# Up biases of a mixture of experts: products on TensorE, or a broadcast and adds on GpSimd

## The chip, the cores and the metric

The kernel runs on one core of a Trainium2 chip. The metric is the device time of one execution in microseconds: the median of three runs.

## The reference

One layer of an encoder for 512 rows of 1024 features: layer norm, a mixer (latent attention beside a gated recurrence, one output projection), layer norm, and a mixture of 32 experts of which each row takes four. All in float32.

```python
hb = xb @ w_up[e] + b_up[e]                     # 1024 -> 2048
glu, lin = jnp.split(hb, 2, axis=-1)
glu = jnp.minimum(glu, 7.0)
lin = jnp.clip(lin, -7.0, 7.0)
act = glu * jax.nn.sigmoid(1.702 * glu) * (lin + 1.0)
y = act @ w_down[e] + b_down[e]                 # 1024 -> 1024, then times the gate, added to the row
```

The change touches how `b_up[e]` comes into `hb`, and how the rows of `w_down[e]` lie on the partitions.

## The kernel before, in words

Some 345 us go to the mixer, the second norm and the routing. The expert stage follows: for each expert one block of 128 slots, 32 for each quarter of the rows (a loop for what overflows a quarter runs as often as the counts ask for). The rows of a block are gathered from DRAM by an indirect DMA on GpSimd's queue (`fetch`, line 388), transposed by TensorE and split into a high part in fp32r and the rest (`x_T`). The weights are split in the same way: `Stream` loads chunks of 128x2048 float32 (1 MB) on SyncE's queue into raw buffers (`w_raw`; four, four and `RAW_C` of two, ten in all), ScalarE copies the high part (line 88) and VectorE subtracts it from the raw chunk (line 90, raw and high part both in SBUF), with four buffers for each part. A raw buffer that VectorE has read is loaded again at once. A product of full precision is then three products of TensorE (lines 410 to 412): high by high, high part of x by low part of w, low by high.

An expert has eight chunks of `w_up` (four sums of 128x512 in PSUM, twelve products a chunk) and four of `w_down` (two sums, twelve products a chunk; a chunk has two rows of `w_down` to a partition, p and 128 + p of its 256). The biases `b_up` of all experts lie in SBUF as three bfloat16 pieces to a row (`prepare_up`, at the end of the mixer); a product with a column of ones at the expert's three rows starts each of the four up sums (`bias_mm`, line 415).

The order of the work on every engine in the expert stage is written out by hand: `experts` runs up of expert e, then down of expert e - 1. Beside the up chunks `turn` goes forward by one step a chunk (transposes of the activations of e - 1, then of the rows of e + 1, then places and gates of the next four experts now and then); beside the down chunks `halves` does the activations of e (ScalarE reads the sums for the sigmoid and for lin + 1, VectorE reads the first again for the gate, line 439, then clamps and multiplies, lines 444 and 445). After each chunk, `ahead` splits the chunk three further on. `finish` scales the down sums on ScalarE (line 473) and adds them to a DRAM table with an indirect DMA on GpSimd (line 474). When all loads have been issued, each `ahead` also takes one step of `final_tiles`, which borrows free raw buffers, has GpSimd split `b_down` and the gates (lines 497 to 502), and has TensorE transpose the latter (line 514). An instruction waits for its operands on its engine's queue, and all behind it wait too.

Of the kernel before, what the change touches and what calls it, by code (L numbers as in the profile page):

```python
# [21 lines left out]
NE = 32  # L22
# [99 lines left out]
class Consts:  # L122
    def __init__(self, nc, pool, tmp):
        self.mhalf = pool.tile([128, 4], F32, name="mhalf")
        nc.gpsimd.memset(self.mhalf, -0.5)
        nc.scalar.copy(tmp.tile([128, 4], F32, name="act_table"), self.mhalf)
        jp = tmp.tile([128, 128], I32, name="jp")
        nc.gpsimd.iota(jp, pattern=[[1, 128]], base=0, channel_multiplier=-1)
        self.ident = pool.tile([128, 128], F32, name="ident")
        nc.vector.tensor_scalar(self.ident, jp, 0.0, None, op0=ALU.is_equal)  # L130
        self.before = pool.tile([128, 128], BF, name="before")
        nc.vector.tensor_scalar(self.before, jp, 0.0, None, op0=ALU.is_gt)
        self.ones = pool.tile([128, 128], BF, name="ones")
        nc.vector.memset(self.ones, 1.0)

        self.base = pool.tile([128, 1], F32, name="base")
        for b in range(NB):
            nc.gpsimd.memset(self.base[SLB * b:SLB * b + SLB, :], BIG + 128.0 * b)
        self.slots = pool.tile([128, 128], F32, name="slots")
        nc.gpsimd.iota(self.slots, pattern=[[1, 128]], base=-int(BIG), channel_multiplier=0,  # L140
                       allow_small_or_imprecise_dtypes=True)
        self.pcol = pool.tile([128, 1], F32, name="pcol")
        nc.gpsimd.iota(self.pcol, pattern=[[0, 1]], base=0, channel_multiplier=1,
                       allow_small_or_imprecise_dtypes=True)
        self.ecol = pool.tile([128, NE], F32, name="ecol")
        nc.gpsimd.iota(self.ecol, pattern=[[1, NE]], base=0, channel_multiplier=0,
                       allow_small_or_imprecise_dtypes=True)
        self.erow = pool.tile([128, NE], F32, name="erow")
        t = tmp.tile([128, NE], F32, name="sel_t")
        nc.vector.tensor_scalar(self.erow, jp[:, :NE], 0.0, None, op0=ALU.is_equal)  # L150
        for r in (1, 2):
            nc.vector.tensor_scalar(t, jp[:, :NE], -float(r * NE), None, op0=ALU.is_equal)
            nc.vector.tensor_add(self.erow, self.erow, t)
        self.erow_b = pool.tile([128, NE], BF, name="erow_b")
        nc.vector.tensor_copy(self.erow_b, self.erow)


class Moe:
    def __init__(self, tc, ctx, a, cst, ne=NE):
# [7 lines left out]
        self.bias = ctx.enter_context(tc.tile_pool(name="moe_bias", bufs=1)).tile([128, 2048], BF, name="bias")  # L167
# [21 lines left out]
    def load_consts(self, pool):  # L189
        nc, a = self.nc, self.a  # L190
        self.wr = pool.tile([128, 8, NE], F32, name="w_router", bufs=1)
# [22 lines left out]
    @staticmethod  # L214
    def dn_src(w, k):
        return [(lambda t: t.rearrange("p (k n) -> p k n", k=2),
                 w[256 * k:256 * (k + 1), :].rearrange("(k p) n -> p k n", p=128))]
# [104 lines left out]
    def prepare_up(self, tmp):  # L322

        nc = self.nc
        nc.gpsimd.memset(self.bias[96:128], 0.0)

        bq = tmp.tile([128, 512], F32, name="prep_b")
        for q in range(4):
            nc.scalar.dma_start(bq[32 * q:32 * q + 32], self.a["b_up"][0][:, 512 * q:512 * q + 512])
        for r in range(3):  # L330
            pt = tmp.tile([128, 512], BF, name=f"prep_p{r}")
            nc.scalar.copy(pt, bq)
            if r < 2:
                nc.vector.tensor_sub(bq, bq, pt)
            for q in range(4):
                nc.scalar.dma_start(self.bias[32 * r:32 * r + 32, 512 * q:512 * q + 512],
                                    pt[32 * q:32 * q + 32, :])

    def open(self, ctx, h1, h1_pool):
# [12 lines left out]
        self.l_bufs = [self.xp.tile([128, 512], F32, name=f"act_l{i}", bufs=1) for i in range(2)]  # L352
        self.oh = self.xp.tile([128, NB, GRP, SLB], F32, name="oh", bufs=1)
# [60 lines left out]
    def bias_mm(self, ps, sel, j):  # L414
        self.nc.tensor.matmul(ps, sel, self.bias[:, 512 * j:512 * j + 512], start=True, stop=False)

    def up_begin(self, sel):
        ps = [self.ps_up.tile([128, 512], F32, name="ps_up_t") for _ in range(4)]
        for j in range(4):
            self.bias_mm(ps[j], sel, j)  # L420
        return ps

    def up_chunk(self, ps, x, w, k):
        wh, wl = w
        xh, xl = (p[:, k, :] for p in x)
        for j in range(4):
            s = slice(512 * j, 512 * j + 512)
            self.mm3(ps[j], xh, xl, wh[:, s], wl[:, s], k == 7)

    def act0(self, ps, h):  # L430

        nc = self.nc
        nc.scalar.activation(self.u_bufs[h], ps[h], AF.Sigmoid, scale=SW_ALPHA)
        nc.scalar.activation(self.l_bufs[h], ps[2 + h], AF.Copy, bias=1.0)  # L434

    def act1(self, ps, h):

        u = self.u_bufs[h]
        self.nc.vector.scalar_tensor_tensor(u, ps[h], LIMIT, u, op0=ALU.min, op1=ALU.mult)
# [7 lines left out]
    def act_T(self, h):  # L447

        nc, ah, al = self.nc, self.ah, self.al
        p = self.ps_tr.tile([128, 4, 128], F32, name="ps_tr", tag="tr")  # L450
        for i in range(4):
            nc.tensor.transpose(p[:, i, :], self.l_bufs[h][:, 128 * i:128 * i + 128], self.c.ident)  # L452
# [122 lines left out]
    def sel_of(self, e):  # L575
        return self.c.erow_b[:, e:e + 1].to_broadcast([128, 128])

    def experts(self, out):
# [17 lines left out]
        def halves(ps):  # L596

            self.act0(ps, 0)
            self.act1(ps, 0)
            yield  # L600
            self.act0(ps, 1)
            self.act1(ps, 1)
            yield
            self.act2(0)
            yield
            self.act2(1)
            yield

        def turn():

            if e:
                t = [self.act_T(h) for h in range(2)]
                next(t[0])
# [5 lines left out]
                yield  # L619
# [14 lines left out]

        slots(0)
# [5 lines left out]
        for e in range(ne + 1):  # L641
            first = e == 0
            steps = turn()
            if e < ne:
# [3 lines left out]
                ps_up = self.up_begin(self.sel_of(e))  # L648
# [36 lines left out]
    def overflow(self, out):  # L685
# [3 lines left out]
        with tc.For_i(0, n, 1) as i:  # L689
# [26 lines left out]
            et = self.xp.tile([128, NE], F32, name="ov_et")  # L716
            nc.vector.tensor_mul(et, self.c.erow, em)
            sc = self.xp.tile([128, 1], F32, name="ov_sc")
            nc.vector.tensor_reduce(sc, et, axis=AX.X, op=ALU.add)
            sel_t = self.xp.tile([128, 1], BF, name="ov_sel")  # L720
            nc.vector.tensor_copy(sel_t, sc)
            sel = sel_t.to_broadcast([128, 128])
# [6 lines left out]
            ps = self.up_begin(sel)  # L729
            for k in range(8):  # L730
                self.up_chunk(ps, self.x[0], chunk(self.up_src(wu, k)), k)
            for h in range(2):
                self.act0(ps, h)
                self.act1(ps, h)
# [680 lines left out]
def run_mixer(tc, ctx, a, c, moe, st):  # L1415
# [152 lines left out]
    with ExitStack() as tst:  # L1568
        moe.prepare_up(pool(tst, "mx_btmp", side="left"))
# [55 lines left out]
RAW_C = 2  # L1625
# [10 lines left out]
def build(tc, a, out):  # L1636
    nc = tc.nc
    with ExitStack() as ctx:
# [5 lines left out]
        st.first = [st.add(*Moe.dn_src(a["w_o"][0], k)) for k in range(4)]  # L1644
# [8 lines left out]
        with ExitStack() as c2:  # L1653
# [44 lines left out]
            def keep_warm():  # L1698

                p = pj.tile([128, 512], F32, name="warm", tag="s")  # L1700
                for _ in range(B_ORDER.count("x")):
                    nc.tensor.matmul(p, c.ones, moe.bias[:, 0:512], start=True, stop=True)
# [33 lines left out]
```

## Time and profile before

| | |
|---|---|
| runs, us | 1536.73, 1534.72, 1534.84; median 1534.84 |
| profiled execution, us | 1533.35, its span 1531.5 |
| busy share of the span | TensorE 96%, VectorE 87%, ScalarE 70%, GpSimd 17% |
| packets on SyncE's queue | 86002, 425.51 MB, 74.1% of 16 engines' span |
| granted TensorE clock | 0.983 of full speed over the span |

The page gives busy time per engine over the span; a stage has to be asked for by itself. Products on TensorE overlap, so the sum of their durations is more than the time that they take, and the distance from one start to the next is what counts. The list of waits gives, for each instruction that found its engine idle, what ended the idle time.

### The profile page before, as it was taken

What the parts mean: (1) busy time and instruction counts of PE and PEld (TensorE: products, weight loads), DVE (VectorE), ACT (ScalarE), POOL (GpSimd) and SP (SyncE); (2) the same over time, 40 slices, a digit from 0 to 9 for tenths busy, and PEclk for the clock granted to TensorE, in tenths of its full rate; (3) what the DMA queues carried; (4) which work ended last, traced back from release to release, by engine and by line L of the source; (5) the groups of instructions that cost most, each with busy time, mean ns of one, the idle gap of its engine ahead of it and who ended that gap; (6) DMA issues with size and microseconds to landing.
All of it is one profiled execution on the core that took longest, in us unless ns stands there. A gap on an engine that the chain in (4) does not pass through costs nothing. (4 is left out here: it accounts for less than half of the span.)

```text
span 1531.5 us, 20026 instructions
## 1 busy us (share of the span) xinstructions
PE 1467.2 (96%) x7368; PEld 1210.5 (79%) x7401; DVE 1325.0 (87%) x1520; ACT 1072.9 (70%) x1148; POOL 259.4 (17%) x251
## 2 busy tenths in 40 slices
PE   7999999979999999999999999999999999999984
PEld 5878998857888888888888888888888888888863
DVE  8867876667999999999999989999999999998975
ACT  4778453336777777777777777777777777777762
POOL 5120413141111111111111111111101111111033
PEclk9999999999999999999999999999999999999997
DMA  5222116376999999999999999999999999999943
GB/s 200 91 76 56 29 51 256 139 262 238 337 362 366 377 364 367 371 373 366 372 374 363 363 372 364 355 383 367 379 357 371 375 367 364 378 368 359 360 150 115
DMA packets 100729, 457.15 MB, mean 298 GB/s; under 512 B 14031, under 2 KB 24696, under 8 KB 67858
## 3 DMA queue, kind: packets, MB, share of 16 engines
q1 hardware_dynamic: 86002, 425.51, 74.1%
q0 software_dynamic: 12672, 29.50, 6.6%
q8 instruction: 60, 0.98, 0.3%
q10 hardware_dynamic: 1952, 0.80, 0.2%
q14 instruction: 43, 0.35, 0.1%
HBM read 447.26 MB, written 24.64 MB: 308 GB/s over the span
## 5 line engine op out<-in xcount | busy, mean ns | idle before, releaser
L90 DVE TENSOR_TENSOR w_lo_t<-w_raw,w_hi_t 128x2048 fp32r<-128x2048 f32 (+1 forms) x392 | 880.8, 2267 | 89.9 <-ACT w_hi_t L88 89.0
L88 ACT CAST w_hi_t<-w_raw 128x2048 fp32r<-128x2048 f32 (+1 forms) x392 | 725.4, 1896 | 13.9 <-DMA w_raw<-in_w_o 12.2
L410 PE MATMUL ps_up_t<-w_hi_t,xh 128*128 128x512 f32 x1024 | 420.1, 410 | 0.0
L412 PE MATMUL ps_up_t<-w_hi_t,xl 128*128 128x512 f32 x1024 | 403.2, 394 | 0.0
L411 PE MATMUL ps_up_t<-w_lo_t,xh 128*128 128x512 f32 x1024 | 399.9, 390 | 0.0
L474 POOL DMA_INDIRECT acc_dram<-h,idx x31 | 95.5, 3081 | 956.4 <-ACT h L473 749.8
L412 PEld LDWEIGHTS ps_up_t<-w_hi_t,xl 128*128 128x128 f32 x1024 | 192.5, 188 | 43.5
L410 PEld LDWEIGHTS ps_up_t<-w_hi_t,xh 128*128 128x128 f32 x1024 | 193.1, 189 | 39.5 <-issue 0.8
L411 PEld LDWEIGHTS ps_up_t<-w_lo_t,xh 128*128 128x128 f32 x1024 | 193.5, 189 | 37.3
L412 PE MATMUL ps_dn_t<-w_hi_t,h 128*128 128x512 f32 x512 | 200.5, 392 | 1.2 <-DVE h L456 1.2
L410 PE MATMUL ps_dn_t<-w_hi_t,h 128*128 128x512 f32 x512 | 200.7, 392 | 0.2 <-ACT h L455 0.2
L411 PE MATMUL ps_dn_t<-w_lo_t,h 128*128 128x512 f32 x512 | 200.6, 392 | 0.0
L412 PEld LDWEIGHTS ps_dn_t<-w_hi_t,h 128*128 128x128 f32 x512 | 97.0, 189 | 21.8 <-DVE h L456 1.6
L410 PEld LDWEIGHTS ps_dn_t<-w_hi_t,h 128*128 128x128 f32 x512 | 96.9, 189 | 20.6 <-ACT h L455 0.4
L411 PEld LDWEIGHTS ps_dn_t<-w_lo_t,h 128*128 128x128 f32 x512 | 96.8, 189 | 20.2
L404 ACT CAST xh<-ps_tr 128x512 fp32r<-128x512 f32 x64 | 37.7, 588 | 94.9 <-PE ps_tr L401 94.7
L455 ACT CAST h<-ps_tr 128x512 fp32r<-128x512 f32 x64 | 37.5, 588 | 79.6 <-PE ps_tr L452 79.6
L473 ACT ACTIVATE h<-ps_dn_t,gate_s 128x512 f32<-128x512 f32 x62 | 42.4, 688 | 65.0 <-PE ps_dn_t L412 65.0
L940 PE MATMUL pj<-mw_hi,hT 128*128 128x256 f32 (+1 forms) x192 | 59.9, 312 | 1.9 <-ACT hT L1061 1.5
L941 PE MATMUL pj<-mw_lo,hT 128*128 128x256 f32 (+1 forms) x192 | 58.0, 303 | 1.1 <-DVE mw_lo L868 1.1
L942 PE MATMUL pj<-mw_hi,hT 128*128 128x256 f32 (+1 forms) x192 | 57.8, 301 | 0.8 <-DVE hT L1063 0.8
L434 ACT ACTIVATE act_l<-ps_up_t 128x512 f32<-128x512 f32 x64 | 38.5, 601 | 23.7 <-PE ps_up_t L412 23.7
(363 smaller groups left out, 1804.8 us busy)
## 6 DMA issues: line engine op xcount, KB each, us to landing
w_raw<-in_w_up SPq DMA_DIRECT2D x256, 1024.0 KB
w_raw<-in_w_down SPq DMA_DIRECT2D x128, 1024.0 KB
mw_raw<-in_w_in SPq DMA_DIRECT2D x16, 512.0 KB
w_raw<-in_w_o SPq DMA_DIRECT2D x4, 1024.0 KB
mw_raw<-in_w_in SPq DMA_DIRECT2D x4, 672.0 KB
h_dram<-x POOLq DMA_DIRECT2D x4, 512.0 KB, 3.5
h<-h_dram POOLq DMA_DIRECT2D x4, 512.0 KB, 10.2
rows_dram<-h POOLq DMA_DIRECT2D x4, 512.0 KB, 4.5
```

The lines of the kernel that those rows point to most:

```text
L88: self.nc.scalar.copy(h[:, s], r[:, s])
L90: self.nc.vector.tensor_sub(l[:, s], r[:, s], h[:, s].bitcast(F32))
L404: nc.scalar.copy(xh[:, s, :], p)
L410: mm(ps, xh, wh, start=start, stop=False)
L411: mm(ps, xh, wl, start=False, stop=False)
L412: mm(ps, xl, wh, start=False, stop=stop)
L434: nc.scalar.activation(self.l_bufs[h], ps[2 + h], AF.Copy, bias=1.0)
L473: nc.scalar.mul(y[:, 512 * n:512 * n + 512], ps[n], gate)
L474: nc.gpsimd.indirect_dma_start(out=self.acc[:, :], out_offset=bass.IndirectOffsetOnAxis(ap=idx[:, :1], axis=0), in_=y, in_offset=None, bou ...
L940: mm(ps, xh, wh, start=start, stop=False, skip_group_check=True)
L941: mm(ps, xh, wl, start=False, stop=False, skip_group_check=True)
L942: mm(ps, xl, wh, start=False, stop=stop, skip_group_check=True)
```

## The change

GpSimd brings in the biases. One row of `b_up` is loaded as four pieces of 512 to partitions 0, 32, 64 and 96 (`bias_row`; the first on ScalarE's queue, the others on GpSimd's, an expert ahead), and GpSimd broadcasts each to 128 partitions (`bias_rows`) behind the gather. The four bias products go, with their tables. ScalarE copies all four up sums to SBUF, GpSimd adds the biases to the copies in place, and the sigmoid and the gate read these. The clamps and products move from the down stage to the first two steps of the next `turn`. A chunk of `w_down` is loaded with rows 2p and 2p + 1 on partition p, so the transposes of the activations read every second element. `RAW_C` is one, for nine raw buffers in all. Where TensorE was kept busy with products of the bias table before the expert stage, it now multiplies ones. The overflow loop changes in the same manner.

```diff
--- before.py
+++ after.py
...
@@ class Consts: the table of expert rows goes
-        self.erow = pool.tile([128, NE], F32, name="erow")
...
-        self.erow_b = pool.tile([128, NE], BF, name="erow_b")
-        nc.vector.tensor_copy(self.erow_b, self.erow)
...
@@ class Moe
-        self.bias = ctx.enter_context(tc.tile_pool(name="moe_bias", bufs=1)).tile([128, 2048], BF, name="bias")
+        self.bias_pool = ctx.enter_context(tc.tile_pool(name="moe_bias", bufs=2))
...
     def load_consts(self, pool):
         nc, a = self.nc, self.a
+        self.brow0 = self.bias_row(a["b_up"][0, 0:1], nc.scalar)
...
     def dn_src(w, k):
+        return [(lambda t: t, w[256 * k:256 * (k + 1), :].rearrange("(p two) n -> p (two n)", two=2))]
+
+    @staticmethod
+    def out_src(w, k):
         return [(lambda t: t.rearrange("p (k n) -> p k n", k=2),
                  w[256 * k:256 * (k + 1), :].rearrange("(k p) n -> p k n", p=128))]
...
-    def prepare_up(self, tmp):
...
+    def bias_row(self, src, queue):
+
+        t = self.bias_pool.tile([128, 512], F32, name="bias_q")
         for q in range(4):
...
+            queue.dma_start(t[32 * q:32 * q + 1, :], src[:, 512 * q:512 * q + 512])
+        return t
+
+    def bias_rows(self, t):
+
+        self.bias = self.xp.tile([128, 2048], F32, name="bias", bufs=1)
+        for q in range(4):
+            self.nc.gpsimd.partition_broadcast(self.bias[:, 512 * q:512 * q + 512], t[32 * q:32 * q + 1, :])
...
+        self.s_buf = self.xp.tile([128, 512], F32, name="act_s", bufs=1)
...
-    def bias_mm(self, ps, sel, j):
-        self.nc.tensor.matmul(ps, sel, self.bias[:, 512 * j:512 * j + 512], start=True, stop=False)
-
-    def up_begin(self, sel):
-        ps = [self.ps_up.tile([128, 512], F32, name="ps_up_t") for _ in range(4)]
-        for j in range(4):
-            self.bias_mm(ps[j], sel, j)
-        return ps
+    def up_begin(self):
+        return [self.ps_up.tile([128, 512], F32, name="ps_up_t") for _ in range(4)]
...
-            self.mm3(ps[j], xh, xl, wh[:, s], wl[:, s], k == 7)
+            self.mm3(ps[j], xh, xl, wh[:, s], wl[:, s], k == 7, start=k == 0)
-
-    def act0(self, ps, h):
-
-        nc = self.nc
-        nc.scalar.activation(self.u_bufs[h], ps[h], AF.Sigmoid, scale=SW_ALPHA)
-        nc.scalar.activation(self.l_bufs[h], ps[2 + h], AF.Copy, bias=1.0)
-
-    def act1(self, ps, h):
-
-        u = self.u_bufs[h]
-        self.nc.vector.scalar_tensor_tensor(u, ps[h], LIMIT, u, op0=ALU.min, op1=ALU.mult)
+    def act0(self, ps):
+
+        nc = self.nc
+        for h in range(2):
+            for j, t in ((h, self.u_bufs[h]), (2 + h, self.l_bufs[h])):
+                if j < 2:
+                    nc.scalar.copy(t, ps[j])
+                else:
+                    nc.scalar.activation(t, ps[j], AF.Copy, bias=1.0)
+                nc.gpsimd.tensor_tensor(t, t, self.bias[:, 512 * j:512 * j + 512], op=ALU.add)
+
+    def act1(self, h):
+
+        u, s = self.u_bufs[h], self.s_buf
+        self.nc.scalar.activation(s, u, AF.Sigmoid, scale=SW_ALPHA)
+        self.nc.vector.scalar_tensor_tensor(u, u, LIMIT, s, op0=ALU.min, op1=ALU.mult)
... act_T
+        l = self.l_bufs[h].rearrange("p (k q two) -> p k two q", k=2, two=2)
         for i in range(4):
-            nc.tensor.transpose(p[:, i, :], self.l_bufs[h][:, 128 * i:128 * i + 128], self.c.ident)
+            nc.tensor.transpose(p[:, i, :], l[:, i // 2, i % 2, :], self.c.ident)
... experts: halves
-            self.act0(ps, 0)
-            self.act1(ps, 0)
-            yield
-            self.act0(ps, 1)
-            self.act1(ps, 1)
-            yield
-            self.act2(0)
-            yield
-            self.act2(1)
+            self.act0(ps)
+            yield
+            yield
+            self.act1(0)
+            yield
+            self.act1(1)
             yield
... experts: turn
                 t = [self.act_T(h) for h in range(2)]
+                self.act2(0)
+                yield
+                self.act2(1)
                 next(t[0])
                 yield
                 next(t[0])
                 next(t[1])
                 yield
                 next(t[1])
-                yield
             if e + 1 < ne:
... experts: the loop over e
+                self.bias_rows(brow)
+                if e + 1 < ne:
+                    brow = self.bias_row(self.a["b_up"][0, e + 1:e + 2], nc.gpsimd)
-                ps_up = self.up_begin(self.sel_of(e))
+                ps_up = self.up_begin()
...
-RAW_C = 2
+RAW_C = 1
```

## Rows read from the trace of the kernel before

**Rows 1.** The page: busy us of each engine (share of the span) and instructions.
```profile
PE 1467.2 (96%) x7368; PEld 1210.5 (79%) x7401; DVE 1325.0 (87%) x1520; ACT 1072.9 (70%) x1148; POOL 259.4 (17%) x251
```

**Rows 2.** Middle of the expert stage: length, busy us per engine, clock, DMA share, GB/s.
```profile
core 0: us, PE busy (x) PEld busy (x) DVE busy (x) ACT busy (x) POOL busy (x), PEclk, DMA share, GB/s
600.00:1320.00 720.00, 718.64 (x3375) 584.59 (x3394) 663.28 (x469) 555.29 (x444) 90.19 (x40) 1.00 0.99 369
```

**Rows 3.** Waits from 500 to 1400 us, longest of ScalarE, VectorE, SyncE: total, times, longest.
```profile
ACT xh L404 <- PE ps_tr L401: 64.9, 51, 1.7
...
DVE w_lo_t L90 <- ACT w_hi_t L88: 67.1, 121, 1.1
...
SPq L75 <- DVE w_lo_t L90: 628.0, 247, 3.6
```

**Rows 4.** GpSimd in order of time, two scatter-adds: start, us, engine, line [idle before].
```profile
733.70 3.00 POOL L474 DMA_INDIRECT acc_dram<-h,idx  x1 [30.24 <-ACT h L473]
...
769.26 3.01 POOL L474 DMA_INDIRECT acc_dram<-h,idx  x1 [30.79 <-ACT h L473]
```

**Rows 5.** TensorE in order of time, from one expert's down to the next one's up.
```profile
732.32 0.39 PE L412 MATMUL ps_dn_t<-w_hi_t,h 128*128 128x512 f32 x1
732.77 0.81 PE L415 MATMUL ps_up_t<-bias,erow_b 128*128 128x512 bf16 x3
...
733.65 0.39 PE L411 MATMUL ps_up_t<-w_lo_t,xh 128*128 128x512 f32 x1
733.88 0.40 PE L412 MATMUL ps_up_t<-w_hi_t,xl 128*128 128x512 f32 x1
```

**Rows 6.** VectorE's groups from 600 to 1320 us: count | busy us, mean ns | idle before.
```profile
L90 DVE TENSOR_TENSOR w_lo_t<-w_raw,w_hi_t 128x2048 fp32r<-128x2048 f32 x243 | 551.3, 2288 | 54.3 <-ACT w_hi_t L88 53.7 <-ACT act_l L434 0.2
L405 DVE TENSOR_TENSOR xl<-ps_tr,xh 128x512 fp32r<-128x512 f32 x41 | 28.0, 683 | 0.0
L445 DVE SCALAR_TENSOR_TENSOR act_l<-h,act_l 128x512 f32<-128x512 f32 x40 | 27.7, 692 | 1.4
...
L444 DVE TENSOR_SCALAR act_l<-act_l 128x512 f32<-128x512 f32 x40 | 16.8, 420 | 0.0
```

**Rows 7.** VectorE, then GpSimd, in order of time from 187 to 192 us.
```profile
188.50 2.42 DVE L868 TENSOR_TENSOR mw_lo<-mw_raw,mw_hi 128x256 fp32r<-128x256 f32 x2
...
191.68 0.41 DVE L868 TENSOR_TENSOR mw_lo<-mw_raw,mw_hi 128x256 fp32r<-128x256 f32 x1
...
189.30 1.34 POOL L1405 TENSOR_TENSOR sq<-sq,a_u 128x512 f32<-128x512 f32 x1
```

**Rows 8.** VectorE and GpSimd in order of time, near the end of the experts.
```profile
1471.01 2.29 DVE L90 TENSOR_TENSOR w_lo_t<-w_raw,w_hi_t 128x2048 fp32r<-128x2048 f32 x1 [1.78 <-ACT w_hi_t L88]
...
1471.22 4.27 POOL L498 TENSOR_TENSOR w_raw<-w_raw 32x1024 fp32r<-32x1024 f32 x1
```

**Rows 9.** VectorE, then GpSimd, in order of time from 217 to 222 us.
```profile
218.56 1.22 DVE L1247 TENSOR_TENSOR QF<-q,f 128x512 f32<-128x512 f32 x1 [0.22 <-PE hg L1318]
...
217.96 1.27 POOL L1404 TENSOR_TENSOR a_u<-at 128x512 f32<-128x512 f32 x1 [0.85 <-DVE at L1395]
219.18 0.52 POOL L1244 MEMSET hsc<- 128x512 f32 x1
```

**Rows 10.** GpSimd's groups over the whole span: a two-input operation and a copy.
```profile
L1121 POOL TENSOR_TENSOR x<-x,b_in 128x1024 f32<-128x1024 f32 x1 | 2.4, 2360 | 0.0
...
L1209 POOL COPY Kc<-kr 128x256 f32<-128x256 f32 x4 | 1.6, 407 | 13.6 <-DVE kr L1188 13.6
```

**Rows 11.** TensorE in order of time, from expert 0's up to expert 1's up.
```profile
370.24 0.39 PE L412 MATMUL ps_up_t<-w_hi_t,xl 128*128 128x512 f32 x1
...
374.91 0.99 PE L410 MATMUL ps_up_t<-w_hi_t,xh 128*128 128x512 f32 x1
```

**Rows 12.** TensorE in order of time, in the last expert's down stage but one.
```profile
1476.68 0.70 PE L514 MATMUL ps_tr<-ident,w_raw 128*96 128x128 f32 x4 [4.74 <-POOL w_raw L502]
```

**Rows 13.** Two stretches of 4 us before the experts, columns as in rows 2.
```profile
252.00:256.00 4.00, 3.05 (x8) 1.87 (x7) 2.36 (x3) 1.90 (x1) 0.80 (x1) 0.50 1.03 410
...
304.00:308.00 4.00, 3.05 (x14) 2.22 (x13) 1.90 (x6) 1.17 (x3) 0.57 (x1) 1.00 1.04 426
```

More of the change, by code (lines that the diff above doesn't have):

```diff
@@ L147, in __init__ @@
                        allow_small_or_imprecise_dtypes=True)
-        self.erow = pool.tile([128, NE], F32, name="erow")
[L149 to L153, printed above, removed]
-        self.erow_b = pool.tile([128, NE], BF, name="erow_b")
-        nc.vector.tensor_copy(self.erow_b, self.erow)
 class Moe:
@@ L319, in overflow_list @@
         nc.sync.dma_start(self.tab_i, tabi)
-    def prepare_up(self, tmp):
-        nc = self.nc
-        nc.gpsimd.memset(self.bias[96:128], 0.0)
-        bq = tmp.tile([128, 512], F32, name="prep_b")
+    def bias_row(self, src, queue):
+        t = self.bias_pool.tile([128, 512], F32, name="bias_q")
         for q in range(4):
[L329 to L337, printed above, removed]
+            queue.dma_start(t[32 * q:32 * q + 1, :], src[:, 512 * q:512 * q + 512])
[4 more added lines that the diff above has]
+            self.nc.gpsimd.partition_broadcast(self.bias[:, 512 * q:512 * q + 512], t[32 * q:32 * q + 1, :])
     def open(self, ctx, h1, h1_pool):
@@ L573, in finish_on_chip @@
             steps[step[0]](int(step[1]))
-    def sel_of(self, e):
-        return self.c.erow_b[:, e:e + 1].to_broadcast([128, 128])
     def experts(self, out):
@@ L633, in turn @@
                 yield from meta(e // GRP + 1)
+        nc = self.nc
+        brow = self.brow0
         slots(0)
@@ L715, in overflow @@
             drain(self.x_T(0))
[L716 to L722, printed above, removed]
             wu = a["w_up"][0][bass.ds(e, 1)].rearrange("o k n -> (o k) n")
@@ L728, in chunk @@
                 return st.get(c)
-            ps = self.up_begin(sel)
+            self.bias_rows(self.bias_row(a["b_up"][0][bass.ds(e, 1)], nc.sync))
+            ps = self.up_begin()
             for k in range(8):
                 self.up_chunk(ps, self.x[0], chunk(self.up_src(wu, k)), k)
+            self.act0(ps)
             for h in range(2):
-                self.act0(ps, h)
-                self.act1(ps, h)
+                self.act1(h)
                 self.act2(h)
@@ L1567, in run_mixer @@
     ats.close()
-    with ExitStack() as tst:
-        moe.prepare_up(pool(tst, "mx_btmp", side="left"))
     qks.close()
@@ L1643, in build @@
         st = Stream(tc)
-        st.first = [st.add(*Moe.dn_src(a["w_o"][0], k)) for k in range(4)]
+        st.first = [st.add(*Moe.out_src(a["w_o"][0], k)) for k in range(4)]
         moe.add_chunks(st)
@@ L1701, in keep_warm @@
                 for _ in range(B_ORDER.count("x")):
-                    nc.tensor.matmul(p, c.ones, moe.bias[:, 0:512], start=True, stop=True)
+                    nc.tensor.matmul(p, c.ones, c.ones[:, None, :].to_broadcast([128, 4, 128]), start=True, stop=True)
                     yield
```

## The prediction

> **What bounds the kernel now.** The page comes first: TensorE is busy for 96% of the span, VectorE for 87%, ScalarE for 70%, GpSimd for 17% [rows 1]. Such shares mix stages, so next comes the middle of the expert stage by itself, 720 us of it: TensorE is busy for 718.64 us at the full granted clock (2.4 GHz), VectorE for 663.28, ScalarE for 555.29, GpSimd for 90.19, and the DMA engines have a share of 0.99 [rows 2]. Third, who waits for whom there: TensorE's own list is empty. ScalarE waits for TensorE's transposes and sums, and no DMA stands in its list; VectorE's main wait is for ScalarE's high parts; SyncE's loads wait for VectorE to be done with a raw buffer [rows 3]. So the loads come in time, and TensorE sets the pace. The scatter-adds start 35.56 us apart [rows 4]: that is one expert. In TensorE's order of time a product follows the last after 0.23 us [rows 5].
>
> VectorE stands close behind. Its 663.28 us are 92% of the stretch, or 32.8 us in each 35.56. By groups [rows 6]: twelve subtractions of 128x2048 for the low parts of the weights (551.3 us / 243 = 2.27 us each, 27.2 in all), two subtractions from PSUM for x and two of the same size for the activations (0.683 each), two gates L439 of about the same size, two clamps (0.420) and two products L445 (0.692). It has 2.8 us left per expert.
>
> **The change: TensorE.** Four bias products per expert go. At the turn of an expert [rows 5], the last down product starts at 732.32 and the second up product at 733.65: 1.33 us for what two steps of 0.23 would do, so the bias products cost 0.87 us. TensorE alone would then need 34.7 us per expert, 28 us less over 32 experts. The transposes of the activations now read every second element; if that doubled their cost it would be under 1 us, and it lies beside what follows.
>
> **ScalarE.** Four evacuations stay four (two sigmoids become copies), and two sigmoids from SBUF come, 1.4 us if they cost what VectorE's operations on 512 elements cost [rows 6], on an engine that is busy for 555.29 us of 720. Hidden. The sigmoids stand two and three chunks of the down stage (12 products of 0.23 us each) behind the evacuations, so the adds that they wait for have 5 to 8 us; behind a late sigmoid, ScalarE's weight copies would be late.
>
> **Moved.** The clamps and products go from the down stage to the first two chunks of the next up stage, 2.2 us of VectorE, and the activations' transposes come one chunk later. The next down stage alone needs them, five chunks on; no one is late.
>
> **GpSimd and VectorE.** This is the costly part. GpSimd gets four adds of 128x512 and four broadcasts per expert, and GpSimd has 31 us idle of 35.56 (it is busy for 90.19 / 720 of it). But the trace shows that the two engines exclude each other. At 188.50 two subtractions of 128x256 on VectorE, both operands in SBUF, take 2.42 us together, where one takes 0.41 alone: they end 0.28 us after GpSimd's add of 128x512 that started at 189.30 and took 1.34 [rows 7]. It holds the other way too: a subtraction of 1024 elements on GpSimd at 1471.22 takes 4.27 us; VectorE's weight subtraction ran until 1473.30, and GpSimd ended 2.19 us later [rows 8], where 1024 elements take 2.36 without that [rows 10]. So an add of 512, once it may run, holds VectorE's weight subtractions for 2.19 / 2 = 1.1 us: 4.4 us per expert. The add's ScalarE copies come at the start of the down stage, where VectorE has weight subtractions queued without a break. Behind a held subtraction stand the next ones, and TensorE's low-part products wait for them.
>
> The broadcast is not in this trace. Below it lies the memset of 128x512, 0.52 us, above it the add, 1.34; a copy of 128x256 takes 0.41 [rows 7, 9, 10]. I take 0.6 of hold each, 2.4 per expert. They queue on GpSimd right behind the gather, at the second and third chunk of the up stage, and some will run while VectorE does the four subtractions from PSUM, which have one operand in SBUF. I count half as hidden: 1.2 us.
>
> Whether a broadcast holds VectorE at all is open: during the memset at 219.18 a VectorE multiplication of two SBUF operands ended at 219.78, 0.55 us after the GpSimd operation before the memset (217.96 + 1.27), so the memset, which reads nothing, held nothing back [rows 9]. The Trainium skill (SBUF — State Buffer, section "SBUF: two separate sides") has it that a VectorE operation with two SBUF inputs is shut out only by a GpSimd operation that reads SBUF, for the whole of that operation; a broadcast reads one row. By that rule the broadcasts hold and the sum below stands; if they behave as the memset did, it is 1.2 us per expert less and ends at 1594.
>
> VectorE's own work is unchanged in count: L439 now reads SBUF twice. So VectorE's chain per expert is 32.8 + 4.4 + 1.2, and 0.4 that it still waits for ScalarE (it waits 2.8 now, having time): 38.8 us. That passes TensorE's 34.7, and VectorE with GpSimd becomes the bound. 38.8 - 35.56 = 3.24 us for each of 31 experts: +100 us.
>
> **Loads.** Rows of 8 KB to a partition in place of two of 4 KB can only ease the DMA engines, which the longer expert eases anyway. One raw buffer fewer: ten buffers cover ten chunks of 35.56 / 12 = 2.96 us, 29.6 us; nine of 38.8 / 12 = 3.23 cover 29.1. ScalarE waited for no load with the first. I cost both at nothing. The four small DMAs per expert stand on GpSimd's queue behind the broadcasts, with nothing urgent behind them until the adds, 15 us later.
>
> **Ends.** After expert 0 nothing is there to fill TensorE while the sums are read: its last up product started at 370.24, the first of expert 1 at 374.91 [rows 11], of which 0.23 and 0.87 are the product and the biases: 3.6 us of waiting, then some products at the lower clock. Now ScalarE's four copies alone free the sums, without VectorE: 4 us gained, all told. The preparation of the bias pieces ran beside TensorE's projections, and the first b_up row's four small loads take its place on ScalarE's queue: nothing. At the end, the b_down products' transposes waited 4.74 us for GpSimd [rows 12]; those steps come one chunk later with the adds queued behind them, and the clamps move behind the last down stage: +2 us.
>
> **Sum.** The profiled execution took 1533.35 us, its span 1531.5; the runs' median is 1534.84, 0.1% over. 1533.35 + 100 - 4 + 2 = 1631 us.
>
> **Rivals.** (a) Faster: GpSimd's holds fall where VectorE does not need the second operand from SBUF, and TensorE stays the bound at 34.7: 1533.35 - 28 - 4 = 1501. VectorE's work without the four subtractions from PSUM is 32.8 - 2.7 = 30.1; with 4.4 of adds that is 34.5, which just fits, with the broadcasts 36.9, which does not. So it needs broadcasts that hold nothing and a perfect fit of the adds; it decides at a hold of 4.6 us per expert. Against it: the adds come where no PSUM subtraction is due. (b) The same direction, small: perfect fit with broadcasts that hold, 36.9: 1533.35 + 31 x 1.34 - 2 = 1573. (c) All exposed: adds 1.34, broadcasts 1.34 each, 32.8 + 10.7 = 43.5: 1533.35 + 31 x 7.94 - 2 = 1777. For it: the holds are not chosen by anyone; against it, waiting hides an operation's start-up (2.19 against 2.36). (d) TensorE, now waiting in every chunk, is granted 1.2 GHz for part of the time. At 252 to 256 us it had the 0.50 clock, busy 3.05 of 4 us; at 304 to 308, also busy 3.05 of 4, it kept 1.00 [rows 13]. In the new stage it would be busy 34.7 of 38.8. If a quarter of its work ran at half clock it would need 43.4 us and the time would be 1774. (e) The change of layout or the missing raw buffer starves ScalarE of loads: nothing in the waits speaks for it.
>
> **Chances.** Forecast, VectorE and GpSimd in turn, 0.78 (within it 1573 to 1700, (b) being its lower end); (a) 0.06; between (a) and (b), with the broadcasts free, 0.04; (c) 0.05; (d) 0.06; (e) 0.01. Measured differences under 0.2% can't be told from none here. Below 1531.8 lies (a): faster 0.06. Within 0.2%: 0.02, half of the case between (a) and (b). Slower: the rest, 0.92. The range runs from 1560, just under (b), to 1705.
>
> **What would show it.** Right: TensorE's list of waits in the stage fills with VectorE's low parts; the weight subtraction's mean rises from 2.27 by some 0.3 to 0.5 us, with single ones of 3.3 beside a GpSimd add; GpSimd's adds show 1.3 to 3.5 us each, as they wait in turn; the scatter-adds come 38 to 40 us apart; ScalarE still waits for no load. Wrong: weight subtractions that stay at 2.27 beside GpSimd's adds, a period of 34.7, a granted clock under 1, or ScalarE waiting for raw loads.

## The result: 1790 us, a sixth slower, and the profile after

The changed kernel takes 1790.21 us (median of five runs, 1782.46 to 1793.03) where the kernel before takes 1534.84: a ratio of 1.1659, 95% interval [1.1638, 1.1679]. The forecast was 1631, with a range up to 1705: the direction was right, the size was not. 96 us were forecast and 255 came.

First the page, as in [rows 1]; then the middle of the expert stage, as in [rows 2].

```profile
PE 1537.3 (86%) x7273; PEld 1251.3 (70%) x7273; DVE 1413.9 (79%) x1512; ACT 1103.9 (62%) x1209; POOL 840.2 (47%) x630
```

```profile
600.00:1320.00 720.00, 634.36 (x2764) 507.40 (x2763) 597.01 (x388) 476.04 (x400) 376.57 (x233) 0.94 0.85 307
```

No engine is busy throughout. TensorE has fallen from 718.64 to 634.36 of 720 us, and VectorE, which the forecast made the bound, from 663.28 to 597.01. GpSimd is busy for 376.57 us, about half. So something that is not busy time sets the pace, and the waits have to say what. These are the waits from 500 to 1400 us, the stretch of [rows 3]:

```profile
POOL h L427 <- issue: 208.3, 21, 11.3
POOL bias L330 <- issue: 171.9, 18, 11.3
ACT act_s L432 <- POOL h L427: 160.5, 42, 9.8
DVE h L433 <- ACT act_s L432: 106.7, 21, 7.7
...
PE ps_up_t L404 <- ACT w_hi_t L88: 67.7, 19, 5.8
...
PE ps_up_t L405 <- DVE w_lo_t L90: 44.6, 23, 2.2
...
POOL bias L330 <- DMA xg<-rows_dram,idx: 27.4, 4, 9.2
...
DVE w_lo_t L90 <- DMA w_raw<-in_w_down: 4.2, 6, 0.7
```

Read it from TensorE back to the cause: TensorE waits for ScalarE's high parts, ScalarE stands at the sigmoid (L432) for GpSimd's add, and GpSimd's add waits for "issue", that is, for nothing that the profile shows. GpSimd in order of time, one expert, as in [rows 4]:

```profile
1027.99 3.81 POOL L470 DMA_INDIRECT acc_dram<-h,idx  x1 [0.62 <-ACT h L469]
1032.10 2.25 POOL L382 DMA_INDIRECT xg<-rows_dram,idx  x1 [0.30 <-issue]
1043.86 8.88 POOL L330 PARTITION_BROADCAST bias<-bias_q  x4 [9.51 <-issue]
1052.58 2.16 POOL L323 DMA_DIRECT2D bias_q<-in_b_up  x4
1064.65 1.25 POOL L427 TENSOR_TENSOR h<-h,bias 128x512 f32<-128x512 f32 x1 [9.90 <-issue]
1065.87 1.26 POOL L427 TENSOR_TENSOR act_l<-act_l,bias 128x512 f32<-128x512 f32 x1
1067.09 1.72 POOL L427 TENSOR_TENSOR h<-h,bias 128x512 f32<-128x512 f32 x1
1068.78 3.33 POOL L427 TENSOR_TENSOR act_l<-act_l,bias 128x512 f32<-128x512 f32 x1
1072.73 3.81 POOL L470 DMA_INDIRECT acc_dram<-h,idx  x1 [0.61 <-ACT h L469]
```

From one scatter-add to the next are 44.74 us in this expert (43.6 in the mean of 30). GpSimd waits for another engine for 0.6 of them and 24.4 are work; nearly all the rest are two empty stretches, 9.51 us ahead of the first broadcast and 9.90 ahead of the first add. ScalarE has copied the sums long before (its fourth copy starts at 1053.23). At the start of each empty stretch the trace holds two records of GpSimd's sequencer by the name of MODIFY_POOL_CONFIG (1034.61 and 1054.81), 130 in the whole trace against 2 in that of before. They stand wherever GpSimd goes from a broadcast to an add or back. By their name GpSimd changes its program there (a library of such operations); the run with one program for both, below, puts that to the test. Such a change is called a reload from here on. The groups of GpSimd and of VectorE from 600 to 1320 us (count | busy, mean ns | idle before):

```profile
L330 POOL PARTITION_BROADCAST bias<-bias_q x68 | 123.7, 1917 | 160.0 <-issue 132.6 <-DMA xg<-rows_dram,idx 27.4
L427 POOL TENSOR_TENSOR act_l<-act_l,bias 128x512 f32<-128x512 f32 x32 | 73.7, 2304 | 0.0
...
L427 POOL TENSOR_TENSOR h<-h,bias 128x512 f32<-128x512 f32 x32 | 48.2, 1508 | 160.1 <-issue 160.1
```

```profile
L90 DVE TENSOR_TENSOR w_lo_t<-w_raw,w_hi_t 128x2048 fp32r<-128x2048 f32 x202 | 478.8, 2387 | 39.5 <-ACT w_hi_t L88 36.8 <-DMA w_raw<-in_w_down 2.1
L433 DVE SCALAR_TENSOR_TENSOR h<-h,act_s 128x512 f32<-128x512 f32 x32 | 45.9, 1435 | 78.4 <-ACT act_s L432 78.4
```

160.0 us ahead of 17 experts' broadcasts and 160.1 ahead of 16 experts' adds: 9.4 and 10.0 us per expert. Of the first, 27.4 us are put down to the gather's landing and not to "issue". The exclusion that the forecast was about is there too (adds of 1.25 us that take up to 3.33, the weight subtraction at 2387 ns against 2288), but it is not what decides.

### The profile page after: what moved, and what is told of

Its sections match the earlier page's. It is cut to its first block, busy times and chain, and to the rows that moved or that the text cites. A ratio compares the mean times of both kernels' runs of the same rounds, so it can differ in the third digit from the quotient of the medians.

```text
span 1780.7 us, 20403 instructions
## 1 busy us (share of the span) xinstructions
PE 1537.3 (86%) x7273; PEld 1251.3 (70%) x7273; DVE 1413.9 (79%) x1512; ACT 1103.9 (62%) x1209; POOL 840.2 (47%) x630
## 5 line engine op out<-in xcount | busy, mean ns | idle before, releaser
L90 DVE TENSOR_TENSOR w_lo_t<-w_raw,w_hi_t 128x2048 fp32r<-128x2048 f32 (+1 forms) x392 | 919.1, 2362 | 76.8 <-ACT w_hi_t L88 70.9
L404 PE MATMUL ps_up_t<-w_hi_t,xh 128*128 128x512 f32 x1024 | 443.8, 433 | 101.7 <-ACT w_hi_t L88 96.8
L405 PE MATMUL ps_up_t<-w_lo_t,xh 128*128 128x512 f32 x1024 | 434.5, 424 | 64.1 <-DVE w_lo_t L90 64.1
L406 PE MATMUL ps_up_t<-w_hi_t,xl 128*128 128x512 f32 x1024 | 427.4, 417 | 0.0
L330 POOL PARTITION_BROADCAST bias<-bias_q x128 | 239.0, 1966 | 299.5 <-issue 252.9
L427 POOL TENSOR_TENSOR h<-h,bias 128x512 f32<-128x512 f32 x64 | 95.6, 1493 | 311.9 <-issue 287.6
L433 DVE SCALAR_TENSOR_TENSOR h<-h,act_s 128x512 f32<-128x512 f32 x64 | 93.0, 1454 | 171.8 <-ACT act_s L432 171.8
L432 ACT ACTIVATE act_s<-h 128x512 f32<-128x512 f32 x64 | 40.4, 630 | 233.1 <-POOL h L427 230.1
L427 POOL TENSOR_TENSOR act_l<-act_l,bias 128x512 f32<-128x512 f32 x64 | 145.8, 2278 | 0.0
L470 POOL DMA_INDIRECT acc_dram<-h,idx x31 | 116.7, 3763 | 23.1 <-ACT h L469 18.8
L451 ACT CAST h<-ps_tr 128x512 fp32r<-128x512 f32 x64 | 37.6, 588 | 126.0 <-PE ps_tr L448 126.0
L398 ACT CAST xh<-ps_tr 128x512 fp32r<-128x512 f32 x64 | 37.6, 587 | 69.4 <-PE ps_tr L395 69.3
## 6 DMA issues: line engine op xcount, KB each, us to landing
h<-h_dram POOLq DMA_DIRECT2D x4, 512.0 KB, 10.4
```

The costliest lines, as they stand in the source:

```text
L90: self.nc.vector.tensor_sub(l[:, s], r[:, s], h[:, s].bitcast(F32))
L330: self.nc.gpsimd.partition_broadcast(self.bias[:, 512 * q:512 * q + 512], t[32 * q:32 * q + 1, :])
L398: nc.scalar.copy(xh[:, s, :], p)
L404: mm(ps, xh, wh, start=start, stop=False)
L405: mm(ps, xh, wl, start=False, stop=False)
L406: mm(ps, xl, wh, start=False, stop=stop)
```

## The experiments

Each is the changed kernel with the edit shown, unless it says otherwise; "..." stands for lines left out. Theory A is the reload of GpSimd's program, B the exclusion from SBUF.

**Two more reloads.**

```diff
@@ bias_rows: the loop over the four pieces
...
+            if q == 1:
+                self.nc.gpsimd.tensor_tensor(self.tiny, self.c.pcol, self.c.pcol, op=ALU.add)
```

> The changed kernel with one more GpSimd operation per expert, an add of 128x1 (well under 0.5 us of work) between the second and the third broadcast. Theory A: it makes GpSimd change its program twice more per expert, 9 to 10 us each time, all in GpSimd's closed chain: 43.4 + 18 to 20 = 62 us per expert, 2340 to 2420 us in all. Rival B (exclusion from SBUF): an operation of one element per partition holds VectorE for 0.1 us or so: under 1 us per expert, less than 1830.

2226.97 us, 437 more than the changed kernel and below what A gave: one element per partition costs 14 us per expert. GpSimd in order of time:

```profile
1027.64 1.54 POOL L330 PARTITION_BROADCAST bias<-bias_q  x2 [8.49 <-issue]
1039.63 0.18 POOL L332 TENSOR_TENSOR tiny<-pcol 128x1 f32<-128x1 f32 x1 [10.46 <-issue]
1048.53 1.48 POOL L330 PARTITION_BROADCAST bias<-bias_q  x2 [8.71 <-issue]
...
1059.40 1.25 POOL L430 TENSOR_TENSOR h<-h,bias 128x512 f32<-128x512 f32 x1 [7.39 <-issue]
```

The tiny add takes 0.18 us and has 10.46 ahead of it and 8.71 behind. B falls as the main cause: it has no price for that. A gave 18 to 20 us per expert. It came to less, for the broadcasts, no longer beside weight subtractions, fell to 0.8 us each, and the stretch ahead of the first add to 7.4.

**Adds without broadcasts, broadcasts without adds, neither.**

```diff
@@ e2_adds: the loop over e
-                self.bias_rows(brow)
+                if first:
+                    self.bias_rows(brow)
@@ e3_bcast: act0; e1_none has this and no bias_rows and bias_row in the loop
-                nc.gpsimd.tensor_tensor(t, t, self.bias[:, 512 * j:512 * j + 512], op=ALU.add)
```

> The changed kernel, but the biases are broadcast for expert 0 alone and these serve all experts (the other experts' own biases are left out of the result). The four adds per expert stay. Theory A: no alternation of broadcast and add is left in the stage, so no idle GpSimd of 9 us ahead of the adds; VectorE with the adds' holds sets the pace, 32.8 + 4.4 + 0.4 = 37.6 us per expert, 1580 to 1610 us. Rival B: the adds are the larger part of the exclusion (4.4 of 5.6 us as forecast), so most of the 255 us stays: over 1650.

> The changed kernel without the adds (the up biases are left out of the result); rows are loaded and broadcast for every expert. Theory A: no alternation, so no reload; VectorE with the broadcasts' holds needs 32.8 + 1.2 to 2.4 + 0.4 = 34.4 to 35.6 us per expert beside TensorE's 34.7: 1500 to 1535 us. Rival B: the broadcasts hold VectorE by more than forecast (their mean is 1.96 us in the changed kernel): 4 x 1.96 = 7.8, 41 us per expert, over 1650.

> The changed kernel without loading, broadcasting and adding the up biases in the 32 experts (they are left out of the result; all else of the change stays: four ScalarE copies, moved clamps, w_down layout, one raw buffer fewer). Theory A (GpSimd's two reloads of its program per expert, 9 to 10 us each, make its chain of 43.4 us the bound): with GpSimd out of the path TensorE sets the pace again at 34.7 us per expert, 1495 to 1515 us in all. Rival B (VectorE and GpSimd shut each other out of SBUF, forecast 38.8 us per expert): the same, 1495 to 1515. Rival C (something else in the change, such as the layout, the raw buffer or the moved work, is the cause): it stays over 1600.

1599.05 us (1.0420 of before [1.0395, 1.0445]), 1543.21 (1.0052 [1.0037, 1.0066]) and 1522.05 (0.9904 [0.9881, 0.9927]). With adds alone GpSimd is early and waits for the copies, from 600 to 1320 us; the second view is the same stretch by engine, as in [rows 2]:

```profile
L427 POOL TENSOR_TENSOR h<-h,bias 128x512 f32<-128x512 f32 x38 | 106.5, 2802 | 269.0 <-ACT h L424 269.0
```

```profile
600.00:1320.00 720.00, 693.25 (x3157) 553.12 (x3156) 686.25 (x451) 549.00 (x463) 329.44 (x193) 0.99 0.95 352
```

So neither the adds nor the broadcasts alone cost what the two cost together; their alternation does. With adds alone the scatter-adds come 37.3 us apart (mean of 29, the last distance left out), against 37.6 by the forecast's terms. C falls, since without the biases all the rest of the change runs faster than before. But 1522 is more than the forecast's terms give (1501), and the broadcasts alone end a little above their range. In the middle of the stage these cost next to nothing, 35.3 us from one scatter-add to the next where the run without biases has 35.2; most of the 21 us between the two runs lies before the first scatter-add (420.82 against 414.32) and from the last but one on.

**One program for both.**

```diff
@@ experts: once, ahead of the loop over e
+        nc.gpsimd.load_library(library_config._reserved_10)
```

> The changed kernel, whole computation, with one line more: ahead of the expert stage GpSimd loads one library of programs that has both the broadcast and the add, in place of changing between two per expert. Theory A: no reload is left in the stage; what stays is the exclusion between VectorE and GpSimd, 37.5 us per expert as in the run with adds alone and 0.3 to 1.2 for the broadcasts: 1600 to 1645 us, near the 1631 forecast; the adds follow the copies of the sums at once. The gap ahead of the second broadcast stays, since it waits there for the gather to land. If the gaps had another cause than the change of program (the wait for a DMA, the four small loads): over 1700.

1622.38 us (1.0564 [1.0535, 1.0592]), whole computation. The trace holds 4 records of MODIFY_POOL_CONFIG, none of them inside the stage. GpSimd in order of time, one expert:

```profile
1032.95 2.57 POOL L471 DMA_INDIRECT acc_dram<-h,idx  x1 [8.93 <-ACT h L470]
1035.81 2.38 POOL L383 DMA_INDIRECT xg<-rows_dram,idx  x1 [0.30 <-issue]
1038.23 2.95 POOL L331 PARTITION_BROADCAST bias<-bias_q  x1
1046.43 4.13 POOL L331 PARTITION_BROADCAST bias<-bias_q  x3 [5.25 <-DMA xg<-rows_dram,idx]
1050.39 2.04 POOL L324 DMA_DIRECT2D bias_q<-in_b_up  x4
1054.64 1.29 POOL L428 TENSOR_TENSOR h<-h,bias 128x512 f32<-128x512 f32 x1 [2.21 <-ACT h L425]
1055.98 3.25 POOL L428 TENSOR_TENSOR act_l<-act_l,bias 128x512 f32<-128x512 f32 x1
```

The first broadcast follows the gather at once, and the first add waits for ScalarE's copy; ScalarE's sigmoids no longer wait for the adds. This settles it: the same instructions, without the changes of program, take 168 us less. In the middle of the stage the exclusion is left, and VectorE is the bound, as forecast, busy for 705 of 720 us, with weight subtractions of 2558 ns in the mean (before 2288):

```profile
600.00:1320.00 720.00, 688.86 (x3115) 545.87 (x3114) 705.43 (x440) 540.72 (x455) 475.77 (x266) 0.99 0.95 347
```

```profile
L91 DVE TENSOR_TENSOR w_lo_t<-w_raw,w_hi_t 128x2048 fp32r<-128x2048 f32 x228 | 579.0, 2558 | 13.0 <-ACT w_hi_t L89 12.3
```

The second broadcast waits for the gather to land: it starts 10.6 to 13.3 us after the gather (in 9 of 19 experts of the stretch the profile names the landing, in the others "issue"). In the changed kernel the first broadcast starts 10.9 to 12.9 us after it, so this wait lies within the reload ahead of the broadcasts. Which of the two ended last there stays open, but taking only that reload away would not have gained its whole 9.4 us.

**Reloads off the path.** The kernel before, with two tiny operations per expert behind the gather.

```diff
                     self.fetch(e + 2, self.idx[e + 2])
+                self.nc.gpsimd.partition_broadcast(self.tiny, self.c.mhalf[0:1, :])
+                self.nc.gpsimd.tensor_tensor(self.tiny, self.tiny, self.tiny, op=ALU.add)
```

> The kernel before with two tiny operations on GpSimd per expert, behind the gather: a broadcast of 4 elements and an add of 4 (nothing reads them). Theory A: two reloads per expert, 18 to 20 us of GpSimd's 31 idle us, with only the scatter-add behind them, which is due later: no more than 1545 us; a reload costs time only where an operation that others wait for stands behind it. Rival: a reload slows the other engines or the loads by itself; then half or more of the 190 us between the changed kernel and the run with adds alone shows here too: over 1600.

1556.10 us (1.0120 [1.0102, 1.0139]): between what A and the rival gave, 11 us over what A allowed. GpSimd shows both reloads, and a scatter-add that is not late:

```profile
999.92 3.68 POOL L475 DMA_INDIRECT acc_dram<-h,idx  x1 [10.06 <-DVE act_l L446]
1003.90 1.19 POOL L389 DMA_INDIRECT xg<-rows_dram,idx  x1 [0.30 <-issue]
1013.37 0.28 POOL L649 PARTITION_BROADCAST tiny<-mhalf  x1 [8.27 <-issue]
1025.06 0.19 POOL L650 TENSOR_TENSOR tiny<-tiny 128x4 f32<-128x4 f32 x1 [11.41 <-issue]
1035.84 3.12 POOL L475 DMA_INDIRECT acc_dram<-h,idx  x1 [10.59 <-ACT h L474]
```

The period is 35.92 us where it was 35.56 [rows 4] (every fourth is 36.3 where it was 36.0), and TensorE waits for nobody: its up products follow each other after 0.233 us in the mean (0.229 before; down products 0.227 in both). The new tile of 16 bytes had moved the tiles of x by 32 bytes. That is a further theory, D, and it bears on the changed kernel too, where x also stands elsewhere, and on the 1522 above (0.233 as well).

**The place of x.**

```diff
@@ e10_pad: the kernel before, ahead of the tiles oh, xh and xl
+        self.xp.tile([128, 8], F32, name="pad", bufs=1)
@@ e11_align: e1_none, at the same place
+        self.xp.tile([128, 48], F32, name="pad", bufs=1)
```

> The kernel before with one unused tile of 32 bytes per partition ahead of the tiles of x (xh, xl), which moves these by 32 bytes and changes nothing else. The run with two tiny GpSimd operations was 19 us slower than before, and its up products followed each other after 0.2332 us in place of 0.2295; its x tiles had moved by 32 bytes too, as those of the changed kernel have moved by another step. Theory D (the place of x in SBUF against that of the weights sets the pace of the up products): the step is 0.233 here as well and 96 x 0.0037 = 0.36 us per expert are lost, 11 to 15 us: 1545 to 1552. Rival (the reloads themselves slow TensorE): this run takes what the kernel before takes, within 0.2%.

> The run without any up bias (1522.05 us; the biases are left out of the result) with one unused tile of 192 bytes ahead of the tiles of x, which puts these where they stand against the weights in the kernel before. Theory D: the up products' step falls from 0.2333 to 0.229 or less, 0.4 us per expert, and the four bias products' whole 0.87 us per expert show: 1506 to 1511 us. Rival (the step has another cause, such as what else runs beside the products): 1519 to 1525, as without the tile.

1546.88 us (1.0074 [1.0059, 1.0090]) and 1511.28 (0.9834 [0.9815, 0.9852]): D holds, in both directions; the up products' step is 0.233 with the 32 bytes and 0.228 with x put back. Some small tiles of the same pool move along (places, gates, `oh`), but of what an up product reads x alone moves. Scatter-adds with the 32 bytes, then with x put back:

```profile
1029.85 2.96 POOL L475 DMA_INDIRECT acc_dram<-h,idx  x1 [30.75 <-ACT h L474]
...
1065.76 2.96 POOL L475 DMA_INDIRECT acc_dram<-h,idx  x1 [31.15 <-ACT h L474]
```

```profile
1005.88 2.78 POOL L470 DMA_INDIRECT acc_dram<-h,idx  x1 [29.45 <-ACT h L469]
...
1040.52 2.46 POOL L470 DMA_INDIRECT acc_dram<-h,idx  x1 [29.48 <-ACT h L469]
```

35.91 us, as with the reloads and the same shift of the tiles; and 34.64 without biases, against the forecast's 34.7. So reloads that nobody waits for cost nothing that shows in the middle of the stage. The remaining 9 us of the run with reloads lie at the ends: its first scatter-add comes at 423.69 (417.74 with the 32 bytes alone), its last period is 45.36 (41.55).

**The bias by DMA, and the rest of the change alone.**

```diff
@@ e8_dma: the loop over e (its next two lines, the load of the next row, go too)
-                self.bias_rows(brow)
+                self.bias = self.xp.tile([128, 2048], F32, name="bias", bufs=1)
+                nc.gpsimd.dma_start(self.bias, bcast_rows(self.a["b_up"][0, e:e + 1], 2 * F))
```

The second, e4_rest, is the kernel before with the change's `dn_src`, `out_src`, `RAW_C`, `halves`, `turn`, `act1`, `act_T`, and its `act0` without the adds.

> The changed kernel with the whole computation, but the bias row comes to all 128 partitions by one DMA per expert in place of the row's four loads and GpSimd's four broadcasts; GpSimd keeps the four adds. Theory A: GpSimd runs only adds and so reloads nothing: 1599 us as in the run with adds alone, plus what 1 MB more per expert costs the DMA engines, whose share was 0.95 there: 1599 to 1650. If the adds were slow for a reason of their own (and not for the change of program): over 1700.

> The kernel before with all of the change except its core: the four bias products on TensorE stay, while the w_down layout, the missing raw buffer, ScalarE's four copies of the sums, the sigmoid of the copy and the moved clamps are as in the changed kernel. Forecast's terms: start -4, end +2, the rest nothing: 1529 to 1535 us. Against it the run without any bias (1522.05, where the forecast's terms give 1501): if the four products are worth their 0.87 us per expert, 28 us in all, the rest of the change costs 14 to 20 us and this run takes 1548 to 1555.

1592.62 us (1.0364 [1.0344, 1.0384]): adds alone, no reload, and the extra MB costs nothing that shows. 1534.72 (0.9991 [0.9978, 1.0004]): the rest of the change is worth nothing that can be told from none, and the forecast's terms gave 2 us. Here x stands as before (0.229 us per product), and the run without biases at the same place takes 23 us less, so the products are worth the forecast's 28 us within 5.

**A version that beats both.** In the kernel before, with one raw buffer fewer:

```diff
@@ up_begin (self.bl is None in the overflow loop alone)
-        for j in range(4):
+        for j in range(4 if self.bl is None else 2):
...
@@ act0
-        nc.scalar.activation(self.l_bufs[h], ps[2 + h], AF.Copy, bias=1.0)
+        if self.bl is None:
...
+        else:
+            nc.vector.scalar_tensor_tensor(self.l_bufs[h], ps[2 + h], 1.0, self.bl[:, 512 * h:512 * h + 512],
+                                           op0=ALU.add, op1=ALU.add)
...
@@ experts: the loop over e
+                self.bl = self.xp.tile([128, F], F32, name="bias_l", bufs=1)
+                self.nc.gpsimd.dma_start(self.bl, bcast_rows(self.a["b_up"][0, e:e + 1, F:2 * F], F))
```

> A version meant to beat both, whole computation: the kernel before (x tiles in their old place, one raw buffer fewer), in which two of the four bias products stay (those of the gate half, which the sigmoid reads from PSUM) and the other two go: one DMA per expert brings the second half of the bias row to all 128 partitions, and VectorE adds it, with the 1, while it reads the sums from PSUM, in place of ScalarE's copies. GpSimd does nothing but its DMAs, so nothing is reloaded and nothing is held. TensorE per expert 35.52 - 0.43 = 35.1 us, VectorE 32.8 + 2 x 0.69 = 34.2: if these fit beside each other, 1521 to 1526 us. Rival: VectorE with under 1 us to spare, or the 0.5 MB more per expert on the DMA engines, takes the gain back: 1535 or more.

1523.12 us (0.9915 [0.9900, 0.9930]): faster than both, and 0.85% faster than the kernel before. Its scatter-adds come 35.1 to 35.3 us apart (36.0 in every fourth expert), and TensorE is full again with VectorE at 688 of 720 us:

```profile
600.00:1320.00 720.00, 717.56 (x3361) 584.55 (x3380) 687.81 (x514) 543.82 (x408) 75.82 (x60) 1.00 1.01 387
```

## Why the prediction was wrong

- **TensorE, -0.87 us per expert.** Right: 34.64 measured without biases, x in its old place. At the changed kernel's place of x, which the forecast did not look at, some 0.4 of it would be lost again where TensorE sets the pace: e1_none against e11_align, 11 us in all. In the changed kernel itself TensorE does not set the pace.
- **The adds, 4.4 us of hold per expert.** Right in the sum, not in its parts: with adds alone an expert takes 37.3 us, against 37.6. But VectorE's busy time rises from 32.8 to 35.5 us per expert (686.25 of 720), by 2.7 and not 4.4, and it waits for 1.7 us, not 0.4, nearly all for ScalarE's high parts. ScalarE stands at the second sigmoid until VectorE's gate has read the first (`act_s` has one buffer): 89.3 us in the 900 from 500 on.
- **The broadcasts, 1.2 us exposed per expert.** Too much by a third or more: from adds alone to one program for both are 23 us, 0.75 per expert; forecast 37 us. Broadcasts and weight subtractions do exclude each other: a broadcast takes 0.80 us alone and 2.81 behind a weight subtraction, and these take 2327 ns in the mean beside broadcasts alone, 2287 without. By the page named in the forecast (the Trainium skill, SBUF — State Buffer) they had to hold, and the trace agrees.
- **The step that failed: "GpSimd has 31 us idle of 35.56", and the broadcasts and adds priced by their durations alone.** What stands between two kinds of operation was priced at nothing. Two empty stretches per expert, 9.4 us (a reload, with the wait for the gather inside it) and 10.0 us (a reload), filled the 31 us together with the work: 22.8 us busy (376.57 / 16.5 experts), 19.4 empty, 0.9 waiting make 43.1 of 43.6. From there GpSimd, not VectorE, set the pace, and the forecast's sum became that of a kernel without reloads: 1631 against 1622. The 168 us between e7_onelib and the changed kernel come with that one line.
- **That 1622 lies within 9 us of 1631 is in part luck.** In e7_onelib an expert takes 37.9 us (mean of 29), not 38.8, 28 us less over 31 experts: VectorE is held for 4.3 us, not 5.6, and idle for 0.8. The ends took this back. The start was to gain 4 us; the first scatter-add comes 12.5 us later than before (in part by that run's own load of the library), and 9.9 us later in the changed kernel. From the last scatter-add but one on, e7_onelib is 8 us longer, where the end was to cost 2. The first scatter-add before, in e7_onelib and in the changed kernel:

```profile
412.82 3.51 POOL L474 DMA_INDIRECT acc_dram<-h,idx  x1 [50.53 <-DVE act_l L445]
...
425.35 2.60 POOL L471 DMA_INDIRECT acc_dram<-h,idx  x1 [8.93 <-ACT h L470]
...
422.71 3.80 POOL L470 DMA_INDIRECT acc_dram<-h,idx  x1 [0.62 <-DVE h L433]
```

- **What was in sight.** The trace of before has GpSimd adds and no broadcast, and no change of program in its expert stage, so it could not price one. The Trainium skill (GPSIMD Engine Reference, section 2.1, Instruction dispatch) states that the first call into freshly loaded code costs about 6 us and shows no instruction. By it an estimate for GpSimd, with twice 6 per expert, would be 22.8 + 12 + 0.9 = 36 us, still inside VectorE's 38.8; the trace here has 9 to 10, and the measurement decides.
- **"The four small DMAs ... with nothing urgent behind them until the adds, 15 us later."** Wrong in the same place: behind them stood a reload. The first add began 10.4 us after the last row load was issued (1054.26 to 1064.65).
- **Loads, layout, raw buffer, moved clamps, ends: nothing to -2.** Right for the rest of the change by itself (e4_rest), and in the changed kernel ScalarE waits for no load and VectorE for 4.2 us in 900. The ends, once broadcasts and adds stand in them, are not right: see above.
- **Rivals.** (c) with 1777 and (d) with 1774 come near 1790 by number alone. The granted clock of (d) did fall, to 0.94 in the stage and to 0.82 with four reloads, but as an effect: TensorE waits for ScalarE, no product of TensorE stands in the 43.1 us of GpSimd's loop, and with one program the clock is back at 0.99. (c) put 10.7 us of holds on VectorE; it has 4.3 with one program. Rivals (a) to (c) ranked how much of the exclusion shows, and none of them was about GpSimd itself.
- **Signs.** Adds of 1.3 to 3.5 us came (1.25 to 3.33). The weight subtraction rose by 0.1 us, not 0.3 to 0.5; in the expert shown, VectorE waits for the sigmoid while the first add and most of the second run. With one program it rose by 0.27. TensorE's longest wait was for ScalarE's high parts (67.7 us), ahead of the low parts (44.6). The period of 38 to 40 us came in no run: 43.6 with reloads, 37.9 without.

## What to carry to other kernels

Before work is moved to GpSimd, list the kinds of operation that it will run in order of time, not only their durations: each change between kinds that lie in different libraries is an empty stretch of 6 to 12 us here, free where nobody waits behind it and the whole bound where a closed loop runs through it. A trace that lacks such a pair of operations cannot price it, and idle time of an engine is cover only for what can be done within it without such a change. When a tile is added or taken away, see whether the tiles behind it moved.

## What the runs showed of the hardware

- A change of GpSimd's program between broadcast and add left an empty stretch of 6.2 to 11.6 us over 62 in the changed kernel's trace (median 8.8 to the broadcast, 9.7 to the add; the first add's, 15.2, also holds a wait for ScalarE's copies), and recurred at every alternation, also for an add of one element per partition. Where nothing else was waited for (e9_off), it was 6.4 to 12.0 us.
- The place of a matmul's stationary tile in SBUF changed its pace by 2%: by the program's addresses, 0.228 to 0.229 us per product of 512 columns in the mean with x at 2016 bytes past a multiple of 2048 (as the weights are), 0.233 at 0 and at 1824. 96 products per expert make 0.4 us, 11 us in all. The Trainium skill (TensorE: Matmul & The Clock Gate, section "Step-by-step: what each phase is for") states that loading the next tile's weights takes no SBUF read bandwidth from the running product. Here the loads of x take 188 ns in the mean in the kernel before and with the 32 bytes alike, and the pace differs; no run shows by what, nor whether x's own address or its distance from the weights matters.
